# A two-layer decoder trunk on Trainium2: operand offsets in SBUF, rows of y in freed weight slots, a list entry by two comparisons, router weights loaded during the MoE

## The chip, the cores and the metric

The kernel runs on one core of a Trainium2 chip, in one launch. The metric is the time of an execution on the device, in microseconds (us); before and after are compared by their medians. The engines work side by side: TensorE (PE: matmuls and transposes; its weight loads are PEld), VectorE (DVE), ScalarE (ACT) and GpSimd (POOL). SP issues most DMAs, and POOL the indexed ones.

## The reference

```python
h = x                                                   # (1, 1024, 1024) float32
for layer in range(2):
    if layer == 0:
        h = h + conformer_conv(rms_norm(h, ...), ...)   # a = h @ pw1 (1024 x 2048), gate, causal
                                                        # depthwise conv of 31 taps, LayerNorm, silu, @ pw2
    else:
        h = h + hgrn2(rms_norm(h, ...), ...)            # h @ w_in (1024 x 4096), 8 heads, chunked linear
                                                        # recurrence, group norm, gate, @ w_out
    h = h + hier_moe(rms_norm(h, ffn_norm_w[layer]), ...)
return rms_norm(h, final_norm_w)

def hier_moe(h, ...):                                   # 1024 tokens, 32 experts, 2 of 8 in the best group of 4
    gate, expert, token = ...                           # softmax over groups, top-2 softmax in the group
    # rows sorted by expert and padded to blocks of 128; for each block:
    y = (silu(xb @ w_gate[e]) * (xb @ w_up[e])) @ w_down[e]      # 1024 -> 512 -> 1024
    # times its gate, added back at the token's row
```

## The kernel before, in words

All large matmuls are done in three passes: each float32 operand is split into a high and a low part (`wh`, `wl` of a weight, `xh`, `xl` of an activation), and the products high x high, high x low and low x high are summed in PSUM. The high part is a copy by ScalarE (L233), the low part a subtraction by VectorE (L234). The program runs in this order.

- **Layer 0, conv.** The rows are normalised, transposed into `xh`, `xl` (channel by token, pool `axp`), and projected (L1164). The depthwise conv runs on TensorE (L1111), VectorE and GpSimd. The output projection (L331, weights `w20h` to `w23l`, activations `sh`, `sl` in pool `ap`) follows row by row, with the router's logits of layer 0; rows go out to `hD` and, normalised, to `xD`.
- **Routing.** VectorE computes groups, experts, ranks and row lists. `load_router(1)` is written after the MoE, but the order of instructions on each engine is chosen by a scheduler, which puts layer 1's router DMAs (L175 to L178) and their multiplication (L182) here. `past`, `nvf`, `nvt` (L798 to L801) count the blocks beyond the first of each expert. All engines load `nvt` and branch on it (L803): a loop for overflow blocks stands there, which this input does not enter. `place` (L950) marks the rows of the last expert for a later matmul.
- **MoE of layer 0 (L692, L720 to L722).** 33 blocks: one for each of 32 experts, and one more that comes from a list of overflow blocks; the function `entry` (L737 to L760) finds its rows. Weights come as chunks of 1 MB into slots (pools `ring`, `ring3`, `ring4`, `keep`), three halves ahead of their use (`LEAD`). Rows of `xD` are gathered by token (L666), those of y scattered to `yD` (L671). Of the last expert, y is not scattered: `xh`, `xl` (L934, L935) hold its two parts, and TensorE puts them at their rows by `place`.
- **Between the layers (L1290 to L1320).** For each of 8 blocks of 128 rows, y's two parts are read back from `yD` (`read0`), added (L1304, on VectorE for block 0 and on GpSimd for the others), TensorE sums `h` and the last expert's part in PSUM (L960 to L962), VectorE adds both (L1309), the rows are normalised (L295 to L298) and transposed (`sc`). Blocks 0 and 1 use weight slots; 2 to 7 use `my`, of which there are four.
- **Layer 1, HGRN2.** Per head, q and f are projected with tokens as columns (L1343) and the two others row by row (L1365); `w_T` and `w_rows` split their weights (`wqh`, `wql` in L1332, L1333; `wih`, `wil` in L1353, L1354). Then the recurrence, the output projection, MoE 1 (32 blocks) and the last norm.

The inner part of the list entry reads:

```python
for s in range(2):
    for j in range(NT):
        pl1 = mp.tile([P, P], BF, name="pl1")
        nc.vector.tensor_scalar(pl1, iota_r, rel[:, s, j:j + 1], None, op0=OP.is_equal)
        nc.tensor.matmul(tb[:, 0:6], pl1, qv[:, s, j], start=..., stop=...)
```

`tb` is one of the two PSUM buffers `tp`, which the transposes use too.

Of the kernel before, what the change touches and what calls it, by code (L numbers as in the profile page):

```python
# [20 lines left out]
D = 1024  # L21
# [18 lines left out]
YB = 4  # L40
# [19 lines left out]
YDVE = (0,)  # L60
# [19 lines left out]
def trunk(ctx, tc, x, conv_norm_w, conv_pw1_w, conv_pw1_b, conv_dw_w, conv_dw_b, conv_ln_g, conv_ln_b,  # L80
# [27 lines left out]
    wides = [None]  # L108

    def load_w(ap3, pool=None):  # L110
        t = (pool or ring).tile([P, WIDE if pool is wides[0] else 2048], F32, name="wraw")[:, :2048]
        v = t if len(ap3.shape) == 2 else t.rearrange("p (a b) -> p a b", a=ap3.shape[1])
        nc.sync.dma_start(v, ap3)
# [57 lines left out]
    def load_router(l):  # L171
# [10 lines left out]
        nc.vector.tensor_tensor(rw, rw, fcol[:, :, None].to_broadcast([P, KD, 36]), op=OP.mult)  # L182
        r = {"rw": rw, "rb": rb, "lg": const.tile([P, NT, 36], F32, name="lgall"),
# [53 lines left out]
    def split(pool, raw):  # L237

        for i in range(2):
            yield split_half(pool, raw, i)  # L240
# [280 lines left out]
    def moe(l, router, raws, slots, after, last=None, kept=None):  # L521
# [3 lines left out]
        with ExitStack() as held:  # L525
            if NRING2[l]:
                ring2 = held.enter_context(pool_of(f"ring2{l}x", NRING2[l]))
            else:
# [3 lines left out]
            over = ring2  # L532
# [5 lines left out]
                router[k] for k in ("lg", "st", "ohs", "small", "rank", "yidx", "tidx", "listed"))  # L538
            gates = mp.tile([P, NE], F32, name="gates", bufs=1)
# [156 lines left out]
            def mm_in(ps, xt, raw, c):  # L696
                for z, w in enumerate(split(mp, raw)):
                    done = mm_half(ps, xt, w, 4 * c + 2 * z)
                return done
# [24 lines left out]
            def mm_down(pd, ht, raw, c):  # L724
                for z, w in enumerate(split(mp, raw)):
                    mm_down_half(pd, ht, w, 2 * c + z)

# [5 lines left out]
            def entry(i, tag):  # L733
# [46 lines left out]
            def prepare(n):  # L780
                if n >= len(seq):
                    return
# [926 lines left out]
```

## Time and profile before

| | before |
|---|---|
| runs, us | 2354.28 (median of 3; 2352.95 to 2359.45) |
| the profiled execution, us | 2353.6, of which the profile's span is 2351.8 |
| mean granted clock of TensorE | 0.975 of full speed |
| TensorE busy, us | 2226.2 (95%) |
| VectorE busy, us | 1842.5 (78%) |
| ScalarE busy, us | 1458.1 (62%) |
| GpSimd busy, us | 511.8 (22%) |

The span is the time from the first to the last recorded instruction; 1.8 us of the execution lie around it. A matmul of 128x512 is shown with 0.39 us or more, but the next one starts before it ends: what counts is the distance of their starts. The brackets at the end of a row of the timeline say how long the engine had idled before it and what ended that wait.

### The profile page before, as it was taken

How to read it: one execution, taken by the hardware profiler on the slowest of the kernel's cores; microseconds unless marked ns; L12 is line 12 of the kernel's file. 1: busy time of each engine (PE TensorE's matmuls, PEld its weight loads, DVE VectorE, ACT ScalarE, POOL GpSimd, SP SyncE). 2: the span in 40 equal slices, each digit the busy share in tenths (PEclk: the TensorE clock that was granted, in tenths of full speed). 3: DMA queues.
4: the chain of work that ended last, by engine and by line, in shares of the span. 5: the costliest groups of instructions: out<-in, count | busy, mean ns of one | idle time of the engine just before them, and what ended most of it. 6: DMA issues, size and time to landing. Idle time of an engine off the chain costs nothing. (4 is left out here: it accounts for less than half of the span.)

```text
span 2351.8 us, 31895 instructions
## 1 busy us (share of the span) xinstructions
PE 2226.2 (95%) x11825; PEld 1863.3 (79%) x11825; DVE 1842.5 (78%) x2517; ACT 1458.1 (62%) x2035; POOL 511.8 (22%) x310
## 2 busy tenths in 40 slices
PE   7999899699999999998899999989979999999997
PEld 5888777578888878875899999977758888888885
DVE  5898656599999989997376666673479999999996
ACT  5654245378888878884334343332348888888884
POOL 1997301322111111103000000020051111111104
PEclk9999899799999999999999999989979999999999
DMA  5212424499999999987202020205259999999985
GB/s 169 72 55 73 135 90 144 154 338 359 373 377 373 394 354 388 397 323 252 72 14 77 10 82 26 65 32 208 84 201 366 378 374 384 392 391 398 383 329 230
DMA packets 138019, 547.68 MB, mean 233 GB/s; under 512 B 28969, under 2 KB 61921, under 8 KB 87936
## 3 DMA queue, kind: packets, MB, share of 16 engines
q1 hardware_dynamic: 116720, 504.22, 57.5%
q0 software_dynamic: 18720, 33.60, 3.9%
q10 hardware_dynamic: 2416, 7.75, 0.9%
q8 instruction: 95, 1.56, 0.3%
q14 instruction: 68, 0.56, 0.1%
HBM read 519.66 MB, written 60.42 MB: 247 GB/s over the span
## 5 line engine op out<-in xcount | busy, mean ns | idle before, releaser
L234 DVE TENSOR_TENSOR wl<-wraw,wh 128x1024 fp32r<-128x1024 f32 x780 | 932.7, 1229 | 80.6 <-ACT wh L233 71.1
L233 ACT ACTIVATE wh<-wraw 128x1024 fp32r<-128x1024 f32 x780 | 804.3, 1056 | 93.2 <-PE pd L722 77.3
L692 PE MATMUL pu<-wh,xh 128*128 128x512 f32 x520 | 214.6, 413 | 0.0
L692 PE MATMUL pg<-wh,xh 128*128 128x512 f32 x520 | 210.6, 405 | 2.1 <-ACT xh L270 2.1
L692 PE MATMUL pg<-wl,xh 128*128 128x512 f32 x520 | 207.0, 398 | 2.4 <-DVE wl L234 2.2
L692 PE MATMUL pg<-wh,xl 128*128 128x512 f32 x520 | 206.2, 397 | 2.0 <-DVE xl L271 1.9
L720 PE MATMUL pd<-wh,hth 128*128 128x512 f32 x520 | 205.2, 395 | 2.7 <-ACT hth L270 2.7
L692 PE MATMUL pu<-wh,xl 128*128 128x512 f32 x520 | 205.5, 395 | 0.0
L721 PE MATMUL pd<-wl,hth 128*128 128x512 f32 x520 | 204.8, 394 | 0.8 <-DVE wl L234 0.6
L722 PE MATMUL pd<-wh,htl 128*128 128x512 f32 x520 | 204.4, 393 | 0.8 <-DVE htl L271 0.8
L692 PE MATMUL pu<-wl,xh 128*128 128x512 f32 x520 | 203.9, 392 | 0.0
L666 POOL DMA_INDIRECT xg<-xD,tidx x64 | 99.8, 1560 | 463.7 <-PE tp L314 417.5
L671 POOL DMA_INDIRECT yD<-y,yidx x64 | 82.9, 1295 | 497.9 <-ACT y L730 490.2
L1074 POOL TENSOR_TENSOR wraw<-wraw,tap 128x1024 f32<-128x1024 f32 x60 | 155.0, 2584 | 40.5 <-ACT tap L1073 36.1
L1365 PE MATMUL pa<-wih,xh 128*128 128x256 f32 x512 | 147.8, 289 | 5.8 <-ACT q L1346 4.5
L1365 PE MATMUL pa<-wil,xh 128*128 128x256 f32 x512 | 147.6, 288 | 0.0
L1365 PE MATMUL pa<-wih,xl 128*128 128x256 f32 x512 | 147.5, 288 | 0.0
L270 ACT ACTIVATE xh<-tp 128x512 fp32r<-128x512 f32 x146 | 87.0, 598 | 74.3 <-PE tp L314 74.1
L692 PEld LDWEIGHTS pg<-wl,xh 128*128 128x128 f32 x520 | 99.2, 191 | 25.1 <-DVE wl L234 6.8
L692 PEld LDWEIGHTS pg<-wh,xl 128*128 128x128 f32 x520 | 98.8, 190 | 24.3 <-DVE xl L271 3.8
L720 PEld LDWEIGHTS pd<-wh,hth 128*128 128x128 f32 x520 | 98.6, 190 | 23.9 <-ACT hth L270 3.5
L721 PEld LDWEIGHTS pd<-wl,hth 128*128 128x128 f32 x520 | 98.5, 190 | 23.8 <-DVE wl L234 3.0
(492 smaller groups left out, 4874.5 us busy)
## 6 DMA issues: line engine op xcount, KB each, us to landing
wraw<-in_moe_w_gate_dram SPq DMA_DIRECT2D x130, 1024.0 KB, 7.5
wraw<-in_moe_w_up_dram SPq DMA_DIRECT2D x130, 1024.0 KB, 7.6
wraw<-in_moe_w_down_dram SPq DMA_DIRECT2D x130, 1024.0 KB, 7.4
wraw<-in_hgrn_w_in_dram SPq DMA_DIRECT2D x16, 1024.0 KB, 6.6
wraw<-in_conv_pw_w_dram SPq DMA_DIRECT2D x12, 1024.0 KB, 7.0
wraw<-yD SPq DMA_DIRECT2D x10, 1024.0 KB, 9.1
xD<-xn SPq DMA_DIRECT2D x16, 512.0 KB, 2.6
my<-yD SPq DMA_DIRECT2D x6, 1024.0 KB, 6.5
```

Of the source, the lines that this page charges most:

```text
L233: nc.scalar.activation(hi, r, AF.Copy)
L234: nc.vector.tensor_tensor(lo, r, hi, op=OP.subtract)
L270: turned[1] = nc.scalar.activation(hi, ps, AF.Copy)
L666: return nc.gpsimd.indirect_dma_start(out=xg, out_offset=None, in_=xD[l][:, :], in_offset=bass.IndirectOffsetOnAxis(ap=idx, axis=0), bound ...
L671: s = nc.gpsimd.indirect_dma_start(out=yD[l][:, :], out_offset=bass.IndirectOffsetOnAxis(ap=idx, axis=0), in_=y, in_offset=None, bounds_ch ...
L692: done = nc.tensor.matmul(ps, x_[:, kk + k], w_[:, k], start=(kk + k == 0 and x_ is xh and w_ is wh), stop=(kk + k == KD - 1 and x_ is xl))
L720: nc.tensor.matmul(pd[:, ns], hh[:, kk], wh[:, ns], start=(kk == 0), stop=False)
L721: nc.tensor.matmul(pd[:, ns], hh[:, kk], wl[:, ns], start=False, stop=False)
L722: turned[0] = nc.tensor.matmul(pd[:, ns], hl[:, kk], wh[:, ns], start=False, stop=(kk == KF - 1))
L1074: nc.gpsimd.tensor_tensor(res[c], res[c], t, op=OP.add)
L1365: nc.tensor.matmul(pa[:, :256], x_[:, k, js], w_[:, k].rearrange("p z c -> p (z c)"), start=(k == 0 and w_ is wh and x_ is xh), stop=(k == ...
```

## The change

- **Offsets.** A pad of 448 bytes in `axp` and one of 128 bytes in `ap` move tiles. The split tiles of the MoE are made first in their pool, in one order. The addresses within a partition, as bytes past a multiple of 512, moving operand / stationary operand: conv projection (L1164) 480 / 32 before and 32 / 32 after; output projection of layer 0 (L331) 480 / 352 before and 480 / 480 after; both MoEs 480 / 480 before and 352 / 352 after. Layer 1's projection (L1343) has 352 / 352 in both.
- **Rows of y.** All blocks of y's rows are read into slots of `ring4` and `ring3`, four at a time; `my` is gone. SP reads blocks 0 and 1, then two chunks of `w_in`, then blocks 2 to 5, two chunks, and blocks 6 and 7; blocks 4 to 7 wait for the slots of 0 to 3. GpSimd makes all eight adds. The splits for q and f of the first head come after block 2 has been turned (`third`), and TensorE projects q and f of the first half, q and f of the second, and then all rows.
- **List entry.** One comparison of 128x1024 for each half of the list takes the place of eight of 128x128.
- **Router.** The router weights of layer 1 are loaded and multiplied at block 16 of the first MoE.
- **Start of a MoE.** The splits of the first two half chunks are divided in `split_hi` (ScalarE) and `split_lo` (VectorE), and written ahead of the branch on `nvt`; `place` is written behind the last turned product of the MoE. The overflow loop, not entered here, gets tiles of its own.

The core of the diff:

```diff
-    def split_half(pool, raw, i):
-        hi = pool.tile([P, 1024], F32R, name="wh", bufs=WB)
-        lo = pool.tile([P, 1024], F32R, name="wl", bufs=WB)
+    def split_hi(pool, raw, i, bufs=WB):
+        hi = pool.tile([P, 1024], F32R, name="wh", bufs=bufs)
+        lo = pool.tile([P, 1024], F32R, name="wl", bufs=bufs)
         r = raw[:, i * 1024:(i + 1) * 1024]
         nc.scalar.activation(hi, r, AF.Copy)
+        return hi, lo, r
+
+    def split_lo(hi, lo, r):
         nc.vector.tensor_tensor(lo, r, hi, op=OP.subtract)
         return hi, lo
...
+            for nm, n, bufs in (("wh", 1024, WB), ("wl", 1024, WB), ("xh", 1024, 2), ("xl", 1024, 2),
+                                ("hth", 512, HB), ("htl", 512, HB)):
+                mp.tile([P, n], F32R, name=nm, bufs=bufs)
...
                 for s in range(2):
+                    pl1 = mp.tile([P, NT, P], BF, name="pl1", bufs=1)
+                    nc.vector.tensor_tensor(pl1, iota_r[:, None, :].to_broadcast([P, NT, P]),
+                                            rel[:, s, :, None].to_broadcast([P, NT, P]), op=OP.is_equal)
                     for j in range(NT):
-                        pl1 = mp.tile([P, P], BF, name="pl1")
-                        nc.vector.tensor_scalar(pl1, iota_r, rel[:, s, j:j + 1], None, op0=OP.is_equal)
-                        nc.tensor.matmul(tb[:, 0:6], pl1, qv[:, s, j], start=(s == 0 and j == 0),
+                        nc.tensor.matmul(tb[:, 0:6], pl1[:, j], qv[:, s, j], start=(s == 0 and j == 0),
...
             gather(xgs[1], cols(1)[0])
+            parts = [split_hi(mp, *raw_half(n)) for n in range(LEAD - 1)]
...
-            for n in range(LEAD - 1):
-                prepare(n)
             with inorder:
+                ready[0] = split_lo(*parts[0])
                 xt[0] = x_T(xgs[0])
+                ready[1] = split_lo(*parts[1])
             prepare(LEAD - 1)
...
+                    if i == 16 and mid:
+                        mid()
...
-            left = after(mp)
+            with tc.issue_after(turned[2].ins):
+                left = after(mp)
...
             xl = axp.tile([P, KD, T], F32R, name="xl")
+            axp.tile([P, 112], F32, name="pad")
...
+            ap.tile([P, 32], F32, name="pad", bufs=1)
...
+    def next_router():
+        with tc.issue_after(loads[0].ins):
+            later.extend(router_weights(1))
...
-                if j >= len(ys):
-                    ys.append(b0.tile([P, 2 * D], F32, name="my", bufs=YB))
-                    loaded = read0(ys[j], j)
...
-                (nc.vector if j in YDVE else nc.gpsimd).tensor_tensor(y0, y0, y1, op=OP.add)
+                nc.gpsimd.tensor_tensor(y0, y0, y1, op=OP.add)
...
+                if j == 2:
+                    third = turned[2]
+                if j + 4 < NT:
+                    with tc.issue_after(loads[0].ins):
+                        ys.append(read0(ring3 if j > 1 else ring4, j + 4))
...
-            ready = projections(weights(0), first_out, [(0,), (1,)])
+            ready = projections(weights(0, third), first_out, ((0, 0), (1, 0), (0, 1), (1, 1)))
```

Three places show how the order moves. The first is VectorE before the branch of the first MoE, from the lists of token rows to the branch on the block count. Before:

```order
L446 TENSOR_TENSOR yidx<-rows,oob 128x32
L949 TENSOR_TENSOR rel<-tidx,slotbase 128x8
L798 TENSOR_TENSOR past<-tp,slotbase 128x224
L950 TENSOR_TENSOR place<-iota_r,rel 128x1024
L800 TENSOR_REDUCE nvf<-past 128x1
L801 CAST nvt<-nvf 128x1
L802 TENSOR_LOAD nvt
L803 COMPARE_AND_BRANCH
```

After:

```order
L447 TENSOR_TENSOR yidx<-rows,oob 128x32
L805 TENSOR_TENSOR past<-tp,slotbase 128x224
L807 TENSOR_REDUCE nvf<-past 128x1
L808 CAST nvt<-nvf 128x1
L240 TENSOR_TENSOR wl<-wraw,wh 128x1024
L809 TENSOR_LOAD nvt
L810 COMPARE_AND_BRANCH
```

`rel` and `place` have left, and one weight split stands ahead of the branch. The second place is TensorE in the first MoE, where the listed block's rows are found (`pl_...` is the comparison's result, `pd` the down projection of a running block). Before:

```order
L720 MATMUL pd<-wh,hth 128x512
L748 LDWEIGHTS pl_7694
L748 MATMUL tp<-qv,pl_7694 128x6
L748 LDWEIGHTS pl_7697
L748 MATMUL tp<-qv,pl_7697 128x6
L721 MATMUL pd<-wl,hth 128x512
L722 MATMUL pd<-wh,htl 128x512
L720 MATMUL pd<-wh,hth 128x512
L721 MATMUL pd<-wl,hth 128x512
L722 MATMUL pd<-wh,htl 128x512
L720 MATMUL pd<-wh,hth 128x512
L748 LDWEIGHTS pl_7700
```

After:

```order
L726 MATMUL pd<-wh,hth 128x512
L751 LDWEIGHTS pl_7699
L751 MATMUL tp<-qv,pl_7699 128x6
L751 LDWEIGHTS pl_7699
L751 MATMUL tp<-qv,pl_7699 128x6
```

The sixteen pairs, spread over a block and a half, become two runs of eight pairs, twelve large matmuls apart. The third place is VectorE after the last expert of the first MoE (`po`, `st`, `tp` are PSUM tiles with the last expert's rows). Before:

```order
L935 SCALAR_TENSOR_TENSOR xl<-pd,gates,xh 128x1024
L1333 TENSOR_TENSOR wql<-wraw,wqh 128x1024 x2
L1304 TENSOR_TENSOR wraw<-wraw 128x1024
L1309 TENSOR_TENSOR wraw<-po,wraw 128x512 x2
L297 RECIPROCAL ss<-ss 128x1
L298 SCALAR_TENSOR_TENSOR wraw<-wraw,ss,nw 128x1024
```

After:

```order
L946 SCALAR_TENSOR_TENSOR xl<-pd,gates,xh 128x1024
L1330 TENSOR_TENSOR wraw<-po,wraw 128x512 x2
L298 RECIPROCAL ss<-ss 128x1
L1330 TENSOR_TENSOR wraw<-st,wraw 128x512
L1330 TENSOR_TENSOR wraw<-tp,wraw 128x512
L299 SCALAR_TENSOR_TENSOR wraw<-wraw,ss,nw 128x1024
```

The two splits `wql` and the add of y's parts no longer stand ahead of the add to `h`; block 1's add comes before block 0's norm.

## Rows read from the trace of the kernel before

**Rows 1.** The page, part 1: busy time, share of the span, instructions.

```profile
PE 2226.2 (95%) x11825; PEld 1863.3 (79%) x11825; DVE 1842.5 (78%) x2517; ACT 1458.1 (62%) x2035; POOL 511.8 (22%) x310
```

**Rows 2.** Busy time by stretches: PE, PEld, DVE, ACT, POOL; clock, DMA share, GB/s.

```profile
40.00:60.00 20.00, 19.19 (x94) 15.17 (x93) 9.19 (x14) 9.84 (x11) 0.00 (x0) 1.00 0.31 75
60.00:160.00 100.00, 100.00 (x430) 80.62 (x429) 89.36 (x66) 59.85 (x56) 94.77 (x37) 1.00 0.20 68
1067.00:1125.00 58.00, 44.35 (x183) 29.17 (x182) 43.46 (x54) 29.69 (x51) 18.02 (x9) 0.94 0.64 227
1077.20:1080.60 3.40, 2.88 (x5) 1.65 (x6) 1.82 (x4) 1.44 (x3) 3.02 (x2) 0.50 1.02 419
1121.50:1128.40 6.90, 4.58 (x20) 4.29 (x20) 0.48 (x1) 2.81 (x4) 0.00 (x0) 0.51 0.00 0
```

**Rows 3.** Timeline of PE, two pairs: start, us, instruction.

```profile
50.00 0.40 PE L1164 MATMUL pa<-xh,wl 128*128 128x512 f32 x1
...
53.27 0.40 PE L1164 MATMUL pa<-xl,wh 128*128 128x512 f32 x1
...
1110.26 0.39 PE L1343 MATMUL pa<-xh,wqh 128*128 128x512 f32 x1
...
1112.75 0.39 PE L1343 MATMUL pa<-xh,wql 128*128 128x512 f32 x1
```

**Rows 4.** Groups of PE instructions: count, busy us, mean ns, idle before.

```profile
L1164 PE MATMUL pa<-xl,wh 128*128 128x512 f32 x256 | 102.4, 400 | 0.0
...
L331 PE MATMUL po<-w20h,sh 128*128 128x512 f32 x32 | 12.2, 467 | 2.1 <-DVE sh L1241 2.1
...
L692 PE MATMUL pg<-wl,xh 128*128 128x512 f32 x520 | 207.0, 398 | 2.4 <-DVE wl L234 2.2
```

**Rows 5.** Timelines of DVE, ACT, PE, POOL around the first MoE's start.

```profile
436.10 0.46 DVE L182 TENSOR_TENSOR rw<-rw,fcol 128x288 f32<-128x288 f32 x1 [0.89 <-DMA rw<-in_router_exp_w_dram]
...
445.07 1.22 DVE L950 TENSOR_TENSOR place<-iota_r,rel 128x1024 fp32r<-128x1024 f32 x1
...
453.32 2.00 ACT L233 ACTIVATE wh<-wraw 128x1024 fp32r<-128x1024 f32 x2
...
458.51 0.80 PE L692 MATMUL pg<-wh,xl 128*128 128x512 f32 x1 [1.22 <-DVE xl L271]
...
452.10 11.98 POOL L597 TENSOR_SCALAR pl<-iota_r,rank 128x128 bf16<-128x128 f32 x13 [2.50 <-DVEq L803]
```

**Rows 6.** Timeline of PE: four block starts and the list entry.

```profile
800.21 0.39 PE L692 MATMUL pg<-wh,xh 128*128 128x512 f32 x1
...
818.03 0.39 PE L692 MATMUL pg<-wh,xh 128*128 128x512 f32 x1
...
836.46 0.39 PE L692 MATMUL pg<-wh,xh 128*128 128x512 f32 x1
836.69 0.18 PE L748 MATMUL tp<-qv,pl 128*128 128x6 bf16 x1
...
851.53 0.86 PE L314 MATMUL tp<-ident,xg 128*128 128x128 f32 x4 [2.22 <-DVE rowf L556]
...
860.50 0.39 PE L692 MATMUL pg<-wh,xh 128*128 128x512 f32 x1
```

**Rows 7.** Timelines of DVE, PE, POOL between the layers; last, DMA issues (median us).

```profile
1071.22 2.36 DVE L1333 TENSOR_TENSOR wql<-wraw,wqh 128x1024 fp32r<-128x1024 f32 x2 [1.18 <-ACT wqh L1332]
1073.50 3.38 DVE L1304 TENSOR_TENSOR wraw<-wraw 128x1024 f32<-128x1024 f32 x1
...
1077.72 2.07 PE L960 MATMUL po<-wraw,ident 128*128 128x512 f32 x2 [3.15 <-DVE wraw L1309]
...
1122.49 0.58 PE L1365 MATMUL pa<-wih,xh 128*128 128x256 f32 x1 [4.48 <-ACT q L1346]
...
1101.92 2.40 POOL L1304 TENSOR_TENSOR my<-my 128x1024 f32<-128x1024 f32 x1 [16.60 <-DMA my<-yD]
...
my<-yD SPq DMA_DIRECT2D x6, 1024.0 KB, 6.5
```

More of the change, by code (lines that the diff above doesn't have):

```diff
@@ L106, in apool @@
         return tc.alloc_tile_pool(name=name, bufs=bufs, reuse_waits="tile", **kw)
-    wides = [None]
+    wides, loads = [None], [None]
     def load_w(ap3, pool=None):
@@ L519, in first_chunks, with moe @@
         return [load_w(moe_src(l, *keys[i]), pool) for i, pool in enumerate(pools)]
-    def moe(l, router, raws, slots, after, last=None, kept=None):
+    def moe(l, router, raws, slots, after, last=None, kept=None, mid=None):
         with ExitStack() as held:
@@ L694, in mm_half, with over_half @@
                 return done
[L696 to L699, printed above, removed]
+            def over_half(ev, part, i):
+                raw = ring2.tile([P, 2048], F32, name="wraw")[:, :1024] if NRING2[l] else \
+                    rp.tile([P, 1024], F32, name="oraw", bufs=1)
+                nc.sync.dma_start(raw, moe_src(l, ev, part, i // 2)[:, i % 2 * 1024:(i % 2 + 1) * 1024])
+                return split_lo(*split_hi(rp, raw, 0, 1))
             def h_T(pg, pu, name="hh"):
@@ L786, in prepare @@
                     raw_of[key] = get(key)
-                with inorder:
-                    ready[n] = split_half(mp, raw_of[key], z)
+                return raw_of[key], z
+            def prepare(n):
+                if n < len(seq):
+                    half = raw_half(n)
+                    with inorder:
+                        ready[n] = split_lo(*split_hi(mp, *half))
             gather(xgs[0], cols(0)[0])
             gather(xgs[1], cols(1)[0])
+            parts = [split_hi(mp, *raw_half(n)) for n in range(LEAD - 1)]
             cnt = counts()
@@ L808, in moe @@
                 list_rest()
+                rp.release()
+                rp = apool(f"over{l}", 1)
                 with tc.For_i(nb - NE, nv, 1) as it:
@@ L975, in trunk @@
     zD = dram.tile([P, npe, CW], F32, name="zD")
[L976 to L977 removed]
+    ring3 = apool("ring30", 2, side="right")
+    ring4 = apool("ring40", 2, side="right")
     wides[0] = ring4
@@ L1312, in trunk @@
                 rows.append(h)
-            with tc.issue_after(loaded.ins):
+                if j == 2:
+                    third = turned[2]
+                if j + 4 < NT:
+                    with tc.issue_after(loads[0].ins):
+                        ys.append(read0(ring3 if j > 1 else ring4, j + 4))
+                if j == 1:
+                    raws += in_chunks(0, range(2, 4))
+            with tc.issue_after(loads[0].ins):
                 for j, h in enumerate(rows):
                     nc.sync.dma_start(rD[j * P:(j + 1) * P, :], h)
-        bi = apool("b1i", 1)
         kept.release()
         keep.release()
+        ring4.release()
+        ring3.release()
+        bi = apool("b1i", 1)
         hp_ = apool("b2", 1, side="right")
@@ L1369, in proj_rows, with weights, projections @@
                     nc.scalar.activation(dst[:, j, 1], pa[:, P:2 * P], AF.Silu)
-            def weights(hd):
-                return w_T(raws[0], hd % 2), w_T(raws[1], hd % 2), w_rows(raws[2], raws[3], hd % 2)
-            def projections(w, dst, halves):
-                q, f, vg = dst
-                for hs_ in halves:
-                    js_ = [j for hf in hs_ for j in range(4 * hf, 4 * hf + 4)]
-                    if hs_ == (1,):
-                        proj_rows(vg, w[2], js_)
-                    for hf in hs_:
-                        proj_T(q, w[0], hf, AF.Silu)
-                    for hf in hs_:
-                        proj_T(f, w[1], hf, AF.Sigmoid)
-                    if hs_ != (1,):
-                        proj_rows(vg, w[2], js_)
+            def weights(hd, dep=None):
+                with tc.issue_after(dep.ins) if dep else ExitStack():
+                    w = w_T(raws[0], hd % 2), w_T(raws[1], hd % 2)
+                return w + (w_rows(raws[2], raws[3], hd % 2),)
+            def projections(w, dst, parts=((0, 0), (0, 1), (1, 0), (1, 1))):
+                q, f, vg = dst
+                for z, hf in parts:
+                    proj_T((q, f)[z], w[z], hf, (AF.Silu, AF.Sigmoid)[z])
+                proj_rows(vg, w[2], range(NT))
                 return q, f, vg
@@ L1552, in trunk @@
                 o6 = recurrence(hd, *now)
-                ready = projections(w, head_out(hd + 1), [(0, 1)])
+                ready = projections(w, head_out(hd + 1))
             bi.release()
```

60 lines of the change are left out of this document (25 added, 35 removed).

## Prediction, made before the changed kernel had run

> **What bounds the kernel now.** I read the engines' busy shares first. TensorE is busy for 95% of the span, and no other engine comes near [rows 1]. A gain can therefore only come from the 5% in which TensorE idles, from the stretches in which it runs at half clock, or from matmuls that follow each other too slowly. Next I read the busy time by stretches. From 60 to 160 us (the pointwise projections of layer 0) TensorE is busy for all of 100 us. Between the layers, from 1067 to 1125, it is busy for only 44.35 of 58 us. [...] Then I read block starts in the first MoE: 800.21 to 818.03 is 17.82 us, which I take as the period of an undisturbed block [rows 6]. The change leaves such a block as it is, so I price six disturbed places and sum them against the profiled execution's 2353.6 us.
>
> **1. Pads of 448 and 128 bytes.** Nothing is computed differently; only addresses change. In the conv projections (moving operand 480 bytes past a 512-byte line, stationary 32) fourteen matmuls start between 50.00 and 53.27 us: 0.2336 us each. Where both stand at 352, eleven start between 1110.26 and 1112.75: 0.2264 us each [rows 3]. The difference is 7 ns. The former are three groups of 256, that is 768 [rows 4], so at most 768 x 7 ns = 5.4 us. GpSimd is no cause of it: from 40 to 60 us it is not busy at all (0.00) [rows 2]. After 160 us TensorE shares the stage with other waits, so I take 4.0 us. In layer 0's output projection 480 stands against 352; there are twelve groups of 32, 384 matmuls [rows 4]. The bound is 2.7 us; I take 1.5, since it waits more often. The lower bound for both is 0: the trace shows that unlike offsets go with slow starts, not that they cause them. [...]
>
> **2. Router weights and `place` leave the routing chain.** Before the first MoE, VectorE waits 0.89 us for the router weights of layer 1 and multiplies them for 0.46; the next instruction would start some 1.3 us earlier without that. The comparison `place` stands between two steps of the block count and takes 1.22 us [rows 5]. Both go: 2.5 us. They return in covered places. The router's five DMAs are issued on SP behind load 102 of the MoE weights, while VectorE multiplies them after it has split 108, so they have been issued long before; `place` stands ahead of the last weight split, whose matmuls come last of the expert. If either cover were gone, the price would be its own 1.2 to 1.4 us.
>
> **3. First weights of a MoE split before the branch.** Two ScalarE splits (2.00 us) and one VectorE split now run before the count is read. On VectorE the split (1.2 us, as `place` of the same shape) stands behind the count and ahead of the branch, so it gives back 1.2 of the 2.5 us above. After the branch ScalarE no longer has 2.00 us of splits ahead of the first `xh` [rows 5]. So the first MoE should start 2.5 - 1.2 + 2.0 = 3.3 us earlier. The best case is 6: the third matmul, which now comes at 458.51 after another 1.22 us of waiting for `xl` [rows 5], finds `xl` ready and the crossing costs nothing more. The worst case is -2, a loss: the second gather now stands behind the branch, and GpSimd runs thirteen `pl` for 11.98 us there [rows 5]. In the second MoE the second block already waits for GpSimd's chain, so I take 0.3.
>
> **4. List entry by two comparisons.** The blocks that start at 818.03 and 836.46 take 18.43 and 24.04 us, 6.83 more than two undisturbed ones. A wait of 2.22 us for `rowf` ends at 851.53: the transposes need the PSUM buffer that the sixteen small matmuls hold until VectorE has gone round sixteen comparisons [rows 6]. Afterwards there are two comparisons of 128x1024 (the nearest row is `place`, same shape, 1.22 us) and two runs of eight matmuls, and the second run ends before the next block begins, with some 45 large matmuls (10 us) ahead of the transposes that need the buffer. The wait and the half clock behind it go. The sixteen small matmuls stay; one shows 0.18 us [rows 6], so they cost up to 2.9. Net 4.0; bounds 0 and 6.8.
>
> **5. Between the layers.** TensorE loses 58 - 44.35 = 13.65 us by idling from 1067 to 1125, and at half clock about half of each busy stretch, 2.3 us of the last one and 1.4 of one at 1077: 17.4 in all. The chain to the first row is: two splits `wql` (2.36), then the add of the two y rows on VectorE (3.38, from 1073.50), then the add to `h`; TensorE waits 3.15 us for it. Now GpSimd has added rows 0 and 1 before the expert ends, and `wql` is held back until row 2 is turned. TensorE is done with the products of rows 0 and 1 at 1074.6 (3.15 before 1077.72), with row 0 some 2.6 us before. So the add to `h` can follow at about 1072, 5 us earlier. Later, rows 6 and 7 wait for y: GpSimd idles 16.60 us until the fifth load of six into `my` lands, and then TensorE idles 4.48 us for `q` behind the splits of `wih` [rows 7]. New waits arise: row 4's y needs row 0's slot, by my estimate free 7.5 us after that add, at 1079.5, plus 6.5 us of landing [rows 7] and 2.4 of adding [rows 7], so 1088.4, while VectorE would want it at 1086. TensorE waits behind that twice, some 4 us in all; the first `q` waits for row 3, 3 us more; and ScalarE's `wih` splits and table loads stand ahead of the last `xh`, 2 us. So 9 of the 17.4 stay, and I take 8.0 off. Bounds: 3 (only the 3.15 goes) and 15.
>
> **Sum.** 4.0 + 1.5 + 3.3 + 0.3 + 4.0 + 8.0 = 21.1, so 2332.5 in the profiled execution. That one ran 0.7 under the median of the runs (2354.28), so the median should be about **2333**. About 0.3%, 7 us, is what a measurement of this kernel can tell from no change.
>
> **Rivals.**
> A. The offsets cost nothing; the conv's slow starts have another cause, such as its data. For: only unlike pairs in different stages are compared. Against: the regular 7 ns at every start [rows 3]. Without 5.5 us: 2339. [...]
> B. The moved loads come late: the second gather behind the branch takes back the 3.3 us, and row 4's wait doubles and drops the clock again, so that only 3 of the 8 are left. 21.1 - 3.3 - 5 = 12.8: 2342. For: GpSimd's 11.98 us there, and 6.5 us of landing. Against: y rows 6 and 7 come late already before.
> C. Slower. The pads and the tiles that are made first move every MoE operand from 480 past a line to 352. If position counts and not likeness, 520 x 9 = 4680 matmuls [rows 4] could start every 0.2336 instead of 0.2267 us: +32 us against the 21.1, giving 2365. It decides from 21.1 / 4680 = 4.5 ns on. Against: pairs at 352 are the fast ones in layer 1 [rows 3].
> D. The change gains nothing, because TensorE-bound stages behind every gain absorb it: 2354. Against: TensorE itself is the bound, so a lost wait has nothing to hide behind.
>
> **How the numbers follow.** Forecast 0.58, A 0.22, B 0.11, C 0.05, D 0.04. Every case but C and D lies below 2347. The range takes in the bounds of the large terms (all upper ends together would be 36 us, so I go to 32: 2322) and reaches on the other side beyond B, with A on top of it: 12.8 - 5.5 = 7.3, so 2347. Faster 0.89, same 0.06, slower 0.05.
>
> **What would show it.** Conv matmuls start every 0.227 us. The first MoE's third matmul comes 3 us earlier, counted from the end of the stage before. No block of the first MoE but the first eight takes over 20.5 us. From the last expert's product to the first rows product TensorE idles under 10 us. The prediction is wrong if the conv keeps 0.2336 us, if VectorE waits for y rows 4 to 7 as long as TensorE idled before, or if undisturbed blocks no longer take 17.82 us.

## The result, and the profile after

The changed kernel takes 2339.58 us (median of 4 runs, 2338.63 to 2343.48) against 2354.28: a ratio of 0.9925 [0.9911, 0.9939], 14.7 us less. The forecast was 2333, faster, with a range of 2322 to 2347.

Profile of the changed kernel, page, part 1 (it answers to [rows 1]):

```profile
PE 2214.0 (95%) x11825; PEld 1860.3 (79%) x11825; DVE 1835.5 (78%) x2502; ACT 1457.6 (62%) x2035; POOL 515.4 (22%) x311
```

TensorE still bounds the kernel. The totals say little more, so the two traces are compared stage by stage. In the table a stage ends where a named TensorE instruction starts, and each number is the stage's time after the change minus before. The profiled execution (2343.48 us) is the slowest of its four. A second one of the same code (2339.26 us, from the last experiment below) stands beside it.

| stage, ended by | forecast | changed kernel | once more |
|---|---|---|---|
| conv projections, last `pa` | -4.0 | -3.0 | -3.2 |
| output projection of layer 0, its last `po` | -1.5 | +0.4 | -2.5 |
| routing and branch, first `pg` of the first MoE | -3.3 | -4.8 | -4.2 |
| first two blocks of the first MoE | 0 | +3.7 | +2.8 |
| rest of the first MoE, last `pd` | -4.0 | -5.4 | -5.5 |
| between the layers to the last projection of HGRN2 | -8.0 | -2.0 | -2.4 |
| all that follows, with the second MoE | -0.3 | +1.0 | +0.6 |
| sum | -21.1 | -10.1 | -14.3 |

The second execution agrees with the difference of the medians (14.7). Three rows fell furthest short: the first two blocks, the stretch between the layers, and, in one execution only, the output projection.

**The conv.** Timeline of PE in the changed kernel (start, us, instruction), which answers to [rows 3]:

```profile
50.85 0.39 PE L1176 MATMUL pa<-xh,wh 128*128 128x512 f32 x1
...
53.57 0.39 PE L1176 MATMUL pa<-xh,wh 128*128 128x512 f32 x1
```

Twelve starts later it is 2.72 us later: 0.2267 us each, where it was 0.2336.

**The output projection.** Its first transposes of `n` wait for a chain of small VectorE instructions on one number per row. Timeline of the changed kernel, on DVE, POOL and PE:

```profile
282.02 0.16 DVE L287 SCALAR_TENSOR_TENSOR rsy<-rst,rsy 128x1 f32<-128x1 f32 x1
282.22 2.34 DVE L283 SCALAR_TENSOR_TENSOR rst<-rsy,mv 128x1 f32<-128x1 f32 x1
284.59 2.26 DVE L287 SCALAR_TENSOR_TENSOR rsy<-rst,rsy 128x1 f32<-128x1 f32 x1
286.89 0.15 DVE L288 TENSOR_SCALAR rsy<-rsy 128x1 f32<-128x1 f32 x1
287.08 2.07 DVE L1239 SCALAR_TENSOR_TENSOR mv<-mv,rsy 128x1 f32<-128x1 f32 x1
...
282.20 6.93 POOL L1258 TENSOR_TENSOR xr<-xr,b 128x1024 f32<-128x1024 f32 x3 [9.88 <-DVE rsy L287]
...
290.37 1.33 PE L315 MATMUL tp<-ident,n 128*128 128x128 f32 x5 [11.88 <-ACT n L1241]
```

The instructions of 128x1 at L283, L287 and L1239 take 0.16 to 0.22 us elsewhere. Here three of them take 2.07 to 2.34, each about as long as one of GpSimd's three adds (6.93 us together), which began at 282.20. TensorE waits 11.88 us. The same code, once more:

```profile
282.06 0.22 DVE L283 SCALAR_TENSOR_TENSOR rst<-rsy,mv 128x1 f32<-128x1 f32 x1
...
282.70 0.16 DVE L1239 SCALAR_TENSOR_TENSOR mv<-mv,rsy 128x1 f32<-128x1 f32 x1
...
283.66 7.15 POOL L1258 TENSOR_TENSOR xr<-xr,b 128x1024 f32<-128x1024 f32 x3 [11.48 <-DMA xr<-in_x_dram]
...
284.07 1.33 PE L315 MATMUL tp<-ident,n 128*128 128x128 f32 x5 [5.75 <-ACT n L1241]
```

GpSimd's adds begin 0.8 us after the chain's end, nothing in it is stretched, and the wait is 5.75. The 6.1 us between these two executions are thus no property of the change. At the end of the stage 2.9 of them are left (table): later waits are 1.3 us shorter behind the long one, and the half clock ends sooner there (granted clock 0.69 from 290 to 296 us and 1.00 from then on; in the second execution 0.50 from 284 to 296). Of the fourteen profiled executions two show the long wait (this one and experiment 2, 11.77 us) and one a part of it (experiment 4, 7.61); in the other eleven, the kernel before among them, it is 5.74 or 5.75. What decides which instruction is stretched is not shown: of those with one tile as input, the `TENSOR_SCALAR` at L288 takes its 0.15 us amid the others, while a `CAST` `sh<-s` of 128x512 (L1254) takes 1.02 us beside the same adds in the second execution, against 0.43 without them.

**The first MoE's start.** From the last product of the output projection to the block count (`nvt`) it is 20.9 us (21.3 once more) instead of 22.9, and from the count to the first matmul 6.6 us (6.85) instead of 9.46. Part of the second gain lies in the branch: ScalarE and VectorE start again 4.6 us behind it in the kernel before, 0.9 and 1.2 us in the changed one. VectorE's first instruction there (its idle time counts from the count before, from its split after), before:

```profile
452.04 0.19 DVE L571 TENSOR_TENSOR ex<-lgall,small 128x32 f32<-128x32 f32 x1 [5.27 <-DVEq L803]
```

After:

```profile
444.09 0.19 DVE L575 TENSOR_TENSOR ex<-lgall,small 128x32 f32<-128x32 f32 x1 [0.75 <-SPq L810]
```

What comes next, in the timeline of the changed kernel on POOL, DVE and PE:

```profile
449.56 9.99 POOL L601 TENSOR_SCALAR pl<-iota_r,rank 128x128 bf16<-128x128 f32 x6
...
467.45 2.34 POOL L601 TENSOR_SCALAR pl<-iota_r,rank 128x128 bf16<-128x128 f32 x4
469.74 0.17 POOL L652 MEMSET qv<- 128x96 bf16 x1
...
469.94 0.20 DVE L654 TENSOR_SCALAR qv<-tok 128x16 bf16<-128x16 f32 x1 [7.13 <-POOL qv L652]
...
472.07 0.80 PE L696 MATMUL pg<-wl,xh 128*128 128x512 f32 x1 [7.02 <-DVE wl L240]
```

TensorE's wait is put down to a weight split `wl`. But VectorE, ahead of that split, stands 7.13 us before `qv<-tok` until GpSimd has cleared `qv`. The clear takes 0.17 us and stands on GpSimd behind everything that it does for the first two blocks. `qv` is needed some twenty blocks later.

**The list entry.** Timeline of PE in the changed kernel, for [rows 6]:

```profile
814.67 0.39 PE L696 MATMUL pg<-wh,xh 128*128 128x512 f32 x1
...
828.65 0.35 PE L751 MATMUL tp<-qv,pl 128*128 128x6 bf16 x8
...
831.68 0.35 PE L751 MATMUL tp<-qv,pl 128*128 128x6 bf16 x8
...
833.14 0.40 PE L696 MATMUL pg<-wh,xh 128*128 128x512 f32 x1
...
851.01 0.39 PE L696 MATMUL pg<-wh,xh 128*128 128x512 f32 x1
```

The blocks take 18.47 and 17.87 us instead of 18.43 and 24.04; the wait of 2.22 us for `rowf` is gone. The two runs of eight pairs show 0.35 us each.

**Between the layers.** Timeline of the changed kernel, on PE, DVE and POOL:

```profile
1075.88 2.07 PE L971 MATMUL po<-wraw,ident 128*128 128x512 f32 x2 [2.01 <-DVE wraw L1330]
...
1095.38 1.11 PE L315 MATMUL sc<-ident,wraw 128*128 128x128 f32 x4 [4.53 <-DVE xl L272]
...
1111.67 1.25 PE L315 MATMUL sc<-ident,wraw 128*128 128x128 f32 x8 [1.57 <-DVE xl L272]
...
1081.72 2.33 DVE L299 SCALAR_TENSOR_TENSOR wraw<-wraw,ss,nw 128x1024 f32<-128x1024 f32 x1
...
1087.68 2.35 DVE L1363 TENSOR_TENSOR wql<-wraw,wqh 128x1024 fp32r<-128x1024 f32 x2
1089.95 3.37 DVE L299 SCALAR_TENSOR_TENSOR wraw<-wraw,ss,nw 128x1024 f32<-128x1024 f32 x1
...
1094.64 1.28 DVE L272 TENSOR_TENSOR xl<-sc,xh 128x512 fp32r<-128x512 f32 x2
...
1076.92 2.36 POOL L1325 TENSOR_TENSOR wraw<-wraw 128x1024 f32<-128x1024 f32 x1 [11.28 <-DMA wraw<-yD]
1080.60 2.37 POOL L1325 TENSOR_TENSOR wraw<-wraw 128x1024 f32<-128x1024 f32 x1 [1.32 <-DMA wraw<-yD]
1089.49 2.75 POOL L1325 TENSOR_TENSOR wraw<-wraw 128x1024 f32<-128x1024 f32 x1 [6.52 <-PE sc L315]
```

The first transposes `sc` start 12.5 us after the last expert's product (16.0 before). But the last ones start 58.2 after it (50.6 before). The longest wait has moved from `q` [rows 7] to the `xl` of row 3, which stands on VectorE behind the splits `wql` and behind the norms of rows 4 and 5. Row 4's product takes 3.37 us instead of 1.28, beside GpSimd's add at 1089.49. The granted clock, by stretches of the changed kernel, the last two behind the waits of 4.53 and 7.02 us (columns as in [rows 2]):

```profile
1058.00:1116.00 58.00, 45.03 (x178) 29.84 (x177) 39.42 (x52) 29.56 (x50) 16.15 (x8) 0.91 0.58 210
...
1095.38:1099.20 3.82, 3.82 (x11) 3.21 (x12) 2.88 (x6) 2.04 (x4) 2.39 (x1) 0.50 1.03 420
472.07:477.50 5.43, 5.43 (x15) 4.21 (x15) 5.11 (x6) 1.54 (x2) 0.00 (x0) 0.50 0.71 230
```

In the 58 us after the last expert's product TensorE idles 12.97 us (11.28 once more; 13.65 before, [rows 2]). After the two long waits the granted clock is 0.50.

### The profile page after: what moved, and what is told of

Read it like the earlier page. It is cut to its first block, busy times and chain, and to the rows that moved or that the text cites. A ratio compares the mean times of both kernels' runs of the same rounds, so it can differ in the third digit from the quotient of the medians.

```text
span 2341.7 us, 31865 instructions
## 1 busy us (share of the span) xinstructions
PE 2214.0 (95%) x11825; PEld 1860.3 (79%) x11825; DVE 1835.5 (78%) x2502; ACT 1457.6 (62%) x2035; POOL 515.4 (22%) x311
## 5 line engine op out<-in xcount | busy, mean ns | idle before, releaser
L728 PEld LDWEIGHTS pd<-wh,htl 128*128 128x128 f32 x520 | 98.0, 188 | 23.2 <-DVE htl L272 2.4
L696 PEld LDWEIGHTS pu<-wh,xl 128*128 128x128 f32 x520 | 98.1, 189 | 22.6
```

The costliest lines, as they stand in the source:

```text
L696: done = nc.tensor.matmul(ps, x_[:, kk + k], w_[:, k], start=(kk + k == 0 and x_ is xh and w_ is wh), stop=(kk + k == KD - 1 and x_ is xl))
L728: turned[0] = nc.tensor.matmul(pd[:, ns], hl[:, kk], wh[:, ns], start=False, stop=(kk == KF - 1))
```

## The experiments

Ratios are to the kernel before, measured on the same chip. "The stretch" is the time from the last expert's product of the first MoE to the last projection of HGRN2: 559.79 us before, 557.81 and 557.34 in the two executions of the change.

**1. The pads alone.** The kernel before with the two pads and nothing else:

```diff
+            axp.tile([P, 112], F32, name="pad")
...
+            ap.tile([P, 32], F32, name="pad", bufs=1)
```

> The kernel before, with the two pads alone: conv operands 32/32, layer 0's output projection 480/480. Theory (unlike offsets cause the slow starts): conv matmuls start every 0.227 us instead of 0.233, the conv's last projection ends about 3 us earlier, as in the changed kernel, and the total is 3 to 5 us under the kernel before. Rival A (offsets cost nothing): starts stay at 0.233 us, total unchanged within 1 us.

2351.51 us, ratio 0.9984 [0.9973, 0.9995]. The conv ends 3.6 us earlier and the output projection 6.3 us earlier than before. The timeline of PE in this kernel shows twelve starts in 2.72 us:

```profile
50.77 0.39 PE L1165 MATMUL pa<-xh,wl 128*128 128x512 f32 x1
...
53.49 0.39 PE L1165 MATMUL pa<-xh,wl 128*128 128x512 f32 x1
```

Nothing but addresses differs, so the offsets cause the slow starts, and rival A falls.

**2. The old order between the layers.** The changed kernel with the rows of y, `my`, the pools of their slots and the order of projections as before:

```diff
-        ys = [read0(ring4, j) for j in range(2)]
+        ys = [ring.tile([P, 2048], F32, name="wraw") for _ in range(2)]
...
-                nc.gpsimd.tensor_tensor(y0, y0, y1, op=OP.add)
+                (nc.vector if j == 0 else nc.gpsimd).tensor_tensor(y0, y0, y1, op=OP.add)
```

> The changed kernel with the stretch between the layers as before (two rows of y in weight slots, the other six in own tiles, first add on VectorE, splits for q and f not held back, rows projected before the second half of q and f). Theory: between the last expert's product and the end of the first head's projections the change gained nothing (93.0 us before, 93.9 after), and 2 us came later in the recurrence, so this kernel is 0 to 3 us slower than the changed one. Rival, the prediction's step 5: 8 us slower.

2341.7 us, ratio 0.9936 [0.9912, 0.996], not told apart from the change (0.9925). The stretch is 554.89: shorter than with the new order, and 4.9 shorter than before, though its order is that of before. Why is in the timelines. First the kernel before, DVE and POOL, to be read with [rows 7] (the add L1304, 3.38 us at 1073.50):

```profile
1080.01 3.08 DVE L298 SCALAR_TENSOR_TENSOR wraw<-wraw,ss,nw 128x1024 f32<-128x1024 f32 x1
...
1072.96 2.83 POOL L1304 TENSOR_TENSOR my<-my 128x1024 f32<-128x1024 f32 x1 [7.34 <-DMA my<-yD]
```

Then this kernel:

```profile
1066.02 1.22 DVE L1337 TENSOR_TENSOR wraw<-wraw 128x1024 f32<-128x1024 f32 x1
...
1070.38 1.29 DVE L299 SCALAR_TENSOR_TENSOR wraw<-wraw,ss,nw 128x1024 f32<-128x1024 f32 x1
...
1068.09 2.36 POOL L1337 TENSOR_TENSOR my<-my 128x1024 f32<-128x1024 f32 x1 [9.73 <-DMA my<-yD]
```

VectorE's add starts 6.32 us after the last expert's product in both. Before, a row of y had landed by then, and GpSimd was adding; the add took 3.38 and the norm's product 3.08. Here GpSimd's add begins 0.85 us after VectorE's has ended, and the norm's product as GpSimd's ends (1070.45): 1.22 and 1.29. That is 4.0 of the 4.9 us, and the first transposes come 4.0 us earlier. The row lands later because SP issues its read 3.09 us after the last expert's product, where it was 0.19 before. It is no chance of one execution: with the early read (before, and experiment 1) the two take 3.37 or 3.38 and 3.08 us, with the late one (here, and the first kernel of experiment 8) 1.22 and 1.28 or 1.29. Why the read is issued later was not tested. So much of what the new order was to win was a collision, and it goes with the landing of one row. The profiled execution, 2346.95 us, is the slowest of its four, and the gain does not reach its end: the output projection met its collision, and all that follows HGRN2 takes 730.60 us (725.83 in the change).

**3. The splits for q and f held to the last row, or not held.** The changed kernel with one line altered:

```diff
-                if j == 2:
+                if j == NT - 1:
                     third = turned[2]
```

> The changed kernel with the splits for q and f of the first head held until the last row is turned instead of row 2, so that neither the two splits stand ahead of row 3's low part on VectorE nor the 48 matmuls of the first q and f ahead of the transposes of rows 4 to 7 on TensorE. Theory (these two orders are what ate the gain): the last row's transposes come 5 to 10 us earlier after the last expert's product than 58.2 us; but the 48 matmuls (10.9 us) then fill no gaps, so the first head's projections end within 4 us of the changed kernel's. Rival (late rows of y are the bound): the last transposes stay within 2 us and the total is about 10 us slower.

2345.99 us, ratio 0.9968 [0.9956, 0.9979]. The last transposes start 9.7 us earlier after the expert than in the change, so the splits, or the products of q and f that follow them on TensorE, did delay them; this run does not tell the two apart. But the stretch is 564.64, 6.8 longer, and the first head's rows end 5.8 us later (at most 4 was expected): TensorE has less to do meanwhile and idles 16.68 us in the 58 us after the last expert's product. Its timeline:

```profile
1101.31 1.94 PE L315 MATMUL sc<-ident,wraw 128*128 128x128 f32 x8 [5.45 <-issue]
...
1107.12 0.79 PE L1373 MATMUL pa<-xh,wql 128*128 128x512 f32 x1 [3.87 <-DVE wql L1363]
```

And the other way:

```diff
-            ready = projections(weights(0, third), first_out, ((0, 0), (1, 0), (0, 1), (1, 1)))
+            ready = projections(weights(0), first_out, ((0, 0), (1, 0), (0, 1), (1, 1)))
```

> The changed kernel with the splits for q and f of the first head not held back; on VectorE they then stand among rows 0 and 1, where VectorE idles 2.25 us, and no longer ahead of the low part of row 3, for which TensorE waits 4.53 us. Theory (the held splits are what makes that wait): the wait shrinks to about 2 us, the stretch from the last expert's product to the end of HGRN's projections gets 2 to 3 us shorter than the changed kernel's 557.8. Rival (the wait comes from the late row 4 of y and from GpSimd's adds, which stretch VectorE's normalisations from 1.28 to 3.37 us): that stretch stays within 1 us.

2339.05 us, ratio 0.992 [0.9896, 0.9944]; the total is not told apart from the change. The stretch is 554.33, 3.5 shorter. The wait for `xl` only moves to a later row: it is still 4.65 us, where about 2 was expected. The splits now start 9.6 and 12.1 us after the last expert's product, among rows 0 and 1, in whose place VectorE idled for 2.25 us in the change, and the hold costs more than it keeps free.

**4. Adds of rows 4 to 7 on VectorE.** The changed kernel with

```diff
-                nc.gpsimd.tensor_tensor(y0, y0, y1, op=OP.add)
+                (nc.vector if j > 3 else nc.gpsimd).tensor_tensor(y0, y0, y1, op=OP.add)
```

> The changed kernel with the adds of y for rows 4 to 7 on VectorE instead of GpSimd. Theory (a VectorE instruction with two operands in SBUF takes longer when a GpSimd add runs beside it: 2.33 and 3.37 us for two of the norm's products L299 between the layers, where the others take 1.27 or 1.28): every one of the eight L299 products there takes 1.27 to 1.29 us. VectorE gets four adds of 1.2 us for the 3.1 us that it no longer loses, so the wait of TensorE for xl of row 3 (4.53 us in the first execution, 2.83 in the second) falls below 2.5 and the stretch from the last expert's product to the last HGRN projection is 555 to 559 us; total 2337 to 2341. Rival (the long L299 have another cause, such as the landing of y's rows or PSUM): one or two L299 still take 2.3 us or more with no GpSimd add beside them, the wait for xl stays at 2.8 to 4.5, and four adds more on VectorE make the stretch 560 to 563; total 2341 to 2345.

Groups by form, first of the changed kernel, then of this one (count, busy us, mean ns):

```profile
L299 DVE SCALAR_TENSOR_TENSOR wraw<-wraw,ss,nw 128x1024 f32<-128x1024 f32 x8 | 13.4, 1674 | 0.1
```

```profile
L299 DVE SCALAR_TENSOR_TENSOR wraw<-wraw,ss,nw 128x1024 f32<-128x1024 f32 x8 | 10.2, 1280 | 0.1
```

All eight take 1.27 to 1.29 us once no GpSimd add runs beside them, so the adds stretched them. The stretch is 553.44, the shortest of all, though VectorE does four adds more; the wait for `xl` of row 3 is 3.36 us, not below 2.5 as expected. The total is 2336.27 us, ratio 0.9927 [0.9907, 0.9946]: 3 us under the change's median, with the same ratio on its own chip, so the gain of the stretch is shown by the trace and not by the total.

**5. The clear of `qv` ahead of the first gathers.**

```diff
+            if nb > NE:
+                nc.gpsimd.memset(qv, 0.0)
             gather(xgs[0], cols(0)[0])
...
-                nc.gpsimd.memset(qv, 0.0)
```

> The changed kernel with the clearing of qv moved on GpSimd ahead of the first gathers (the scheduler then also keeps the second gather ahead of the branch). Theory (in the changed kernel VectorE waits 7.13 us for that clearing, behind gathers, comparisons and products on GpSimd, and TensorE waits 7.02 us for the weight split behind it): the wait and the half clock after it go, the third block of the first MoE starts 6 to 10 us earlier, total 5 to 9 us under the changed kernel. Rival (GpSimd's chain itself is the bound): another wait for GpSimd takes its place, total within 2 us.

2334.44 us, ratio 0.9915 [0.9896, 0.9934], and once more, beside the change itself:

> The kernel with the early clear of qv alone, once more, beside the one above. Theory: 2334 to 2336 us, 5 us below the changed kernel of the same session, with no wait of 7 us for wl in the second block of the first MoE. Rival (its 2334 of the first session was chance): 2338 to 2340.

2333.71 us, ratio 0.9901 [0.9879, 0.9923]; all five runs (2332.98 to 2334.88) lie under all six of the change (2337.34 to 2341.71). In the second profile of this kernel the first two blocks take 14.18 and 23.25 us instead of 13.28 and 29.04. What TensorE waits for there, in its timeline (POOL, then PE):

```profile
441.22 11.41 POOL L601 TENSOR_SCALAR pl<-iota_r,rank 128x128 bf16<-128x128 f32 x12
...
459.19 0.50 PE L697 MATMUL pg<-wl,xh 128*128 128x512 f32 x1 [0.21 <-DVE wl L240]
...
469.49 0.22 PE L603 MATMUL pd<-qg,pl 128*128 128x96 bf16 x1 [1.43 <-POOL pl L601]
```

The wait of 7 us is gone. The scheduler also put the second gather back ahead of the branch here, so this run does not price the clear apart from the gather's place.

**6. The first splits behind the branch again.**

```diff
-            parts = [split_hi(mp, *raw_half(n)) for n in range(LEAD - 1)]
...
+            for n in range(LEAD - 1):
+                prepare(n)
             with inorder:
-                ready[0] = split_lo(*parts[0])
```

> The changed kernel with the first two halves of the MoE weights split behind the branch, as before; the second gather stays behind the branch. Theory (GpSimd's chain and the wait for qv bound the first two blocks): the first block starts 2 to 4 us later after the count, but the third block at the same time within 1.5 us, total the same. Rival, the prediction's step 3: 2 to 3 us slower in total.

2340.0 us, ratio 0.9932 [0.9912, 0.9952]: as the change. But the edit did not move the splits: the scheduler put two of ScalarE's and one of VectorE's ahead of the branch all the same, which VectorE reaches at 441.95. Timeline of ACT and DVE:

```profile
429.59 1.99 ACT L235 ACTIVATE wh<-wraw 128x1024 fp32r<-128x1024 f32 x2
...
441.22 1.23 DVE L240 TENSOR_TENSOR wl<-wraw,wh 128x1024 fp32r<-128x1024 f32 x1
```

From `nvt` to the first matmul it is 6.8 us (6.6 in the change), the first two blocks take 12.54 and 29.01, and TensorE waits 7.03 us for `wl` there. So neither the theory nor its rival was tested, and no run prices the splits' place.

**7. The list entry by sixteen comparisons again.**

```diff
-                    pl1 = mp.tile([P, NT, P], BF, name="pl1", bufs=1)
-                    nc.vector.tensor_tensor(pl1, ...)
                     for j in range(NT):
+                        pl1 = mp.tile([P, P], BF, name="pl1")
+                        nc.vector.tensor_scalar(pl1, iota_r, rel[:, s, j:j + 1], None, op0=OP.is_equal)
```

> The changed kernel with the list entry's sixteen small comparisons. Theory: the two blocks around it take 18.4 and 24.1 us again instead of 18.47 and 17.87, total 5 to 6.5 us slower than the changed kernel. Rival (the wait moves elsewhere): under 3 us slower.

2346.09 us, ratio 0.9962 [0.9948, 0.9977], which does not overlap that of the change (0.9911 to 0.9939). Timeline of PE:

```profile
832.92 0.39 PE L696 MATMUL pg<-wh,xh 128*128 128x512 f32 x1
...
847.95 0.69 PE L315 MATMUL tp<-ident,xg 128*128 128x128 f32 x4 [2.22 <-DVE rowf L560]
...
855.28 0.39 PE L696 MATMUL pg<-wh,xh 128*128 128x512 f32 x1
```

The block takes 22.36 us instead of 17.87: the wait for `rowf` is back, and with it 4.5 us. About 24.1 was expected, since the same wait cost 6.2 us in the kernel before. There the clock fell behind it and here it did not; why is not shown. The stretches behind the wait, first of the kernel before, then of this one (columns as in [rows 2]):

```profile
851.50:855.00 3.50, 3.46 (x11) 2.91 (x12) 3.27 (x10) 1.55 (x3) 1.01 (x1) 0.56 0.57 166
```

```profile
847.90:851.50 3.60, 3.56 (x18) 3.07 (x19) 3.52 (x11) 2.59 (x4) 1.10 (x1) 1.00 0.72 237
```

The medians differ by 6.5; the rest may be the spread of other places (the first two blocks take 43.56 us here, 42.32 and 41.43 in the change).

**8. Combinations.** The early clear with the old order between the layers (edits 5 and 2):

> The clearing of qv ahead of the first gathers, and the stretch between the layers as before; all else as in the changed kernel. Theory (the new order between the layers costs 2 to 3 us against the old one once all else is as in the changed kernel): 2 to 3 us under the kernel with the early clearing alone (0.9915 of before), that is about 0.990. Rival (the new order gains): 0.992 or above.

2335.57 us, ratio 0.9914 [0.9892, 0.9937], stretch 556.25 against 558.40 with the early clear alone. The totals are not told apart, so this stays open. The early clear with the splits not held (edits 5 and 3):

> The changed kernel with two lines altered: the marks of the list (qv) are cleared ahead of the first gathers, and the splits for q and f of the first head are not held until row 2 is turned. Theory (two separate places, whose gains add): in the first MoE no wait of 7 us for wl, worth about 5 us; between the last expert's product and the last HGRN projection 554 to 556 us instead of 558, worth about 2 to 3. Together 2331 to 2334 us against 2339 to 2341 for the changed kernel of the same session, and 1 to 3 us below the kernel with the early clear alone. Rival (TensorE's later stages, or the vector and GpSimd collisions that differ from execution to execution, take what the second gains): like the early clear alone, 2334 to 2336, with the stretch at 556 to 558.

2332.57 us (2330.62 to 2334.76), ratio 0.9894 [0.9871, 0.9916]. The stretch is 554.94 against 558.13 with the early clear alone in the same session, so the place gains 3.2 us. The total gains 1.1, within its spread. This is the fastest kernel measured, ahead of both before and after.

**9. The change once more.**

> The changed kernel itself once more. Theory that the long wait for n in the output projection of layer 0 comes from when GpSimd's adds xr happen to fall beside small VectorE instructions, which differs between executions of the same code: the wait may be 4 to 6 us or 11 to 12 here, and the last tail-0 matmul comes 3 to 4 us earlier than before or not, while the wait of 7 us for wl at the start of the first MoE stays, since that one comes from the order of GpSimd's instructions. Rival (the long wait is a fixed property of the changed order): 11 to 12 us again. Time 2338 to 2341 in either case.

2340.78 us, ratio 0.9928 [0.9907, 0.9948]. The output projection's wait was 5.75 us this time (shown above). The wait for `wl` was 4.47 us, not 7: it stays, but its size varies too (4.47 to 7.05 us in the eight executions of the change's kind without the early clear).

## Why the prediction was right and wrong

**Right as to the sign and within the range, 6.6 us short in the middle.**

- *Pads.* Right in cause and size: 3.0 to 3.6 us for the conv (forecast 4.0), and 2.5 to 2.7 for the output projection in two executions without the collision (forecast 1.5, bound 2.7). By the mean distance of starts (those under 0.3 us) the output projection went from 0.2328 to 0.2283 us in the changed kernel, which is 1.7 us over its 384 matmuls; the rest of that stage's difference does not lie in the distance of its starts.
- *Rival C* is refuted. The MoE, moved from 480 / 480 to 352 / 352, keeps blocks of 17.83 us (17.82 before) and a median distance of starts of 0.227 us: at these two positions it is likeness that counts.
- *Router weights and `place`* left the routing chain as forecast: the count comes 1.6 to 2.0 us earlier after the output projection (forecast 2.5).
- *The splits ahead of the branch* were mis-sized at the start: from the count to the first matmul 2.6 to 2.9 us were won (forecast 2.0 less 1.2). VectorE's split gave nothing back, for VectorE comes to the branch 0.66 us after the count with it and without it, and the branch was crossed sooner, which the prediction had only in its best case. The execution of experiment 7 has the splits ahead and the old 4.6 us at VectorE's crossing, and 7.79 us from the count to the first matmul; so some 1.7 us may go with the splits and 1.0 with the crossing, read from single executions and not tested. The first MoE thus starts 4.2 to 4.8 us earlier, against 3.3, and its third matmul starts at once behind the second, at 449.65, where it had waited 1.22 us for `xl` [rows 5].
- *The first two blocks* took most of that back, 2.8 to 3.7 us: rival B in part. The prediction watched the second gather behind the branch and GpSimd's thirteen `pl`. It missed that VectorE itself waits for GpSimd, 7.13 us before `qv<-tok`, with the weight splits queued behind. With the clear moved (and the gather back), experiment 5 has the whole at 5 to 7 us less.
- *List entry.* Right: 5.4 us for the rest of the MoE, where the two blocks themselves give 6.1 (forecast 4.0, bound 6.8); experiment 7 shows 4.5 of them by edit, and the rest goes with the half clock that stood behind the wait before. The sixteen small matmuls, priced at up to 2.9 us, cost about 0.7 in two runs of eight. That is why the result is near the bound.
- *Between the layers* is the step that failed: "9 of the 17.4 stay, and I take 8.0 off", and 2.0 to 2.4 came. (Of the 17.4, the 2.3 and 1.4 at half clock are half the busy time of TensorE in the last two stretches of [rows 2].) The chain to the first row did get shorter: the add to `h` comes 3.5 us after the last expert's product (forecast 4.8, before 9.8). The transposes gained less, 3.5 us, as row 1's add to `h` now stands ahead of row 0's norm. Row 4's add ended where it was expected: 21.2 us after the last expert's product, both forecast and measured. But "TensorE waits behind that twice, some 4 us in all" was not how it went. The wait came from VectorE's order, `wql` and the norms of rows 4 and 5 ahead of row 3's `xl`. And 3.38 us for an add was read as its duration, though 2.2 of it were a collision with GpSimd. Such collisions did not go: two norm products took 2.33 and 3.37 us. From the last expert's product to the first rows product TensorE idles 13.09 us (11.39 once more) instead of 12.32. The prediction named "under 10 us" there as a sign of being right, and this sign failed; the conv's distance, the third matmul (5.6 to 6.2 us earlier) and the limit on the blocks came true.
- *The second MoE.* Forecast -0.3, measured +0.6 to +1.0 for all that follows HGRN2. Its first two blocks take 2.5 to 3.0 us longer, with 3.0 us of waiting for GpSimd's `pl`. But the kernel with the pads alone, whose second MoE is that of before, takes 1.8 us longer there, with 3.75 us of that wait; so it is not shown that the change does this.

The sum of the other parts was about right: with the stretch between the layers (5.6 to 6.0 too much) and the first two blocks (2.8 to 3.7 not counted) put right, the forecast would have stood within about 3 us of the median. That is partly luck: routing and the list entry gave 0.9 to 1.5 us more each than forecast, the conv and what follows HGRN2 0.8 to 1.3 us less. The total by itself would have spoken for rival A, which named 2339; only the distance of the starts and experiment 1 tell the two apart.

What stays open: the price of the clear apart from the gather, that of the splits' place, why the branch is crossed sooner, whether the old order between the layers would do as well in the total, and why GpSimd's adds in the output projection begin 1.5 us earlier in one execution than in the other (in the later one the row names the landing of `xr`).

## What to carry to other kernels

Give the two operands of a matmul the same position past a 512-byte line: with float32 operands of 512 columns it was worth 2 to 3% of a start here. Two unlike pairs were slow (480 / 32 with a median distance of starts of 0.233 us, 480 / 352 with 0.232) and three like ones fast (32 / 32, 352 / 352 and 480 / 480, with 0.227 each); whether 512 bytes is the distance that counts was not tested. Before a duration from one row goes into a sum, compare it with the group's other rows of that form; here a row two to three times as long (3.38 us against 1.22) was a collision with an add on GpSimd, and others turned up elsewhere once the order moved (2.33 and 3.37 against 1.28). When work is brought ahead of a branch, follow the queue of the engine that serves both: here a clear of 0.17 us at the end of GpSimd's queue held VectorE, and TensorE behind it, for up to 7 us. And where a scheduler orders the instructions, look in an experiment's trace whether its edit moved anything, before its time is read.

## What the runs showed of the hardware that was not expected

- TensorE's starts follow each other every 0.2336 us when moving and stationary operands stand 480 and 32 bytes past a 512-byte line, and every 0.2267 us at 32 / 32, in the same stage with nothing else changed.
- A VectorE instruction on one number per row (L287) grew from 0.16 to 2.26 us beside GpSimd's adds of 128x1024, an add from 1.22 to 3.38, a norm's product from 1.28 to 3.37. Not all were hit: `TENSOR_SCALAR` of 128x1 (L288) kept its 0.15 us, and the adds to `h` (L1330), with one tile in PSUM, took 0.68 to 0.69 with and without. A `CAST` of 128x512 (L1254) took 1.02 instead of 0.43. No run shows what decides it. The same code was hit in one execution and spared in the next, a difference of 6.1 us in one wait of TensorE.
- Behind the first MoE's branch VectorE and ScalarE started again after 4.2 to 4.6 us in three executions (before, pads alone, experiment 7) and after 0.9 to 1.4 us in the other eleven. No run shows why.
